# A hybrid transformer block on one core: four pieces of work set at other places

## The chip, the cores and the metric

The kernel runs as one program on one core of a Trainium2 chip. The metric is the device time of one execution in microseconds (us); less is better. The engines named below are PE (TensorE, matrix products and transposes), DVE (VectorE), ACT (ScalarE), POOL (GpSimd) and SP (SyncE, which issues nearly all transfers).

## The reference

One block of depth 1 on 512 tokens of 1024 features, in float32. What matters of it:

```python
h = layer_norm(x, emb_ln_g, emb_ln_b)
proj = h @ w_in + b_in
o_dn = gated_delta_rule(q_dn, k_dn, v_dn, beta, g)
y_dn = (rms_norm(o_dn, dn_norm_w) * silu(z)) @ w_dn_o
y_da = (rms_norm(diff_attention_alibi(q, k, v, lam), da_subln_w) * (1 - lam_init)) @ w_da_o
h = layer_norm(alpha * h + (gate_dn * y_dn + gate_da * y_da) @ w_out, ln1_g, ln1_b)
ffn = hierarchical_moe(h, ...)
ple = sigmoid(h @ w_ple_gate + b_ple_gate) * (p @ w_ple_proj)
out = layer_norm(alpha * h + ffn + ple, ln2_g, ln2_b)
```

The mixture has 16 experts, each `silu(h @ gate) * (h @ up)` with 256 inner features and then `@ down`; two experts of one group are taken per token. `p` has 256 features.

## The kernel before, in words

**Products.** A float32 product is written as three float32r products (`mm3`, L287 to L292): high part by high part, low by high, high by low. Each weight is loaded in float32 by SP and split in halves: ACT copies a half into its rounded high part (L265), DVE subtracts that to get the low part (L266). A half is 128x1024 values; one such pair of instructions is called a split here. The list `stream` (L216 to L231) gives the order of all weights from w_in on. `weights(kind, idx, loads, splits)` (L272) asks, when the program uses a weight, that the loads of the next `loads` weights and the splits of the next `splits` halves be issued.

**Order.** The program is written as Python generators whose instructions a scheduler then sets in each engine's queue; an engine works its queue in that order. A few places are pinned: under `strict` the written order holds, `behind(engine)` sets instructions behind all that went before on that engine, `issue_after` behind one instruction.

**The head.** The string `HEAD` (L487) lists tokens in a strict order on PE, DVE, ACT and POOL. Of its tokens, `l1` is one step of the p projection `ple_proj` (L329 to L357): a step makes the products of `p` with `w_ple_proj`, and ACT evicts finished banks as `PPo` (L349 for the first 128 tokens, L356 for the others), from which the three banks of the pool `pg` come free. `a0` and `q1` are the layer norm of the first 128 tokens: ACT's sum (L414) and square (L419). After them come the transposes `psh` of the normed x (L388), whose input DVE finishes at L379.

**The delta rule.** The generator `delta` (inverse, scan, then `dn_out`, L832) is woven step by step with the projections of q and k of the attention (`zqk`). For each of four groups of heads and tokens `dn_out` transposes the scan's output `OR` on PE into a bank `po` (L840), after which `split_o` makes its high and low part. `OR` of the last turn (c = 3) is scaled by `norm_o` (L751): four squares on ACT, then DVE, POOL's power `r` (L209) and DVE's product at L761. Ahead of the last turn `dn_out` waits three steps of the weave.

**The last gate.** `gate_p(c, t)` (L1062) makes the products for the gate of the p projection, four weights PG of 8x262 by four groups of tokens, with `gate_p_use` (L1074) behind them on DVE and ACT. It asks for two splits ahead.

**The experts.** For e = 0 to 15 (loop at L1399) the kernel gathers the rows of x on POOL (L1223), transposes them on PE (`psx`, L1232; ACT and DVE evict them as `xT`, L1234 and L1236), makes the 24 products `pup` of 512 columns with the two weights E(e,0) and E(e,1), gates on ACT and DVE (`eth`, L1261 to L1263), transposes the gated values (`psf`, L1268; evicted as `hT`, L1271 and L1273), and makes 12 products `pdn` with the down weight D(e). ACT evicts these as `y` (L1288) and POOL scatters `y` to `planes` in memory (L1291). There are two buffers of `y`. In `stream` D(e-1) comes behind E(e,0) and E(e,1). An expert has 4 + 2 halves to split; `up` asks for four splits ahead. The last two experts, 14 and 15 (`LAST`), scatter nothing: their results stay on the core (`ykeep`), and `load_planes` reads the planes back behind the last scatter.

Of the kernel before, what the change touches and what calls it, by code (L numbers as in the profile page):

```python
# [20 lines left out]
D = 1024  # L21
NT = 4
NE = 16
# [28 lines left out]
LOADS, SPLITS, PGL, AHEAD = 9, 4, 8, 3  # L52
# [20 lines left out]
def block_kernel(ctx, tc, x, pT, wA, wB, wO, wM, wPG, wPP, wE, wD, cols, rows, consts, out):  # L73
    nc = tc.nc
    PE, DVE, ACT, POOL = nc.tensor, nc.vector, nc.scalar, nc.gpsimd
# [17 lines left out]
    def big(shape, dt=F32, name="big"):  # L93
        return bp.tile([128] + list(shape), dt, name=nm(name), tag="B")
# [10 lines left out]
    def bank(name="ps"):  # L105
        return pt.tile([128, 512], F32, name=nm(name), tag="T")
# [13 lines left out]
    @contextmanager  # L120
    def strict(*engines):

        traced = nc.cur_bb.bb.instructions
        n0 = len(traced)
        yield
        for eng in engines:
            mine = [i for i in traced[n0:] if i.engine == eng.engine]
            for a_, b_ in zip(mine, mine[1:]):
                tc.add_manual_dep(b_, a_.name, mybir.DependencyInfo(mybir.DependencyClass.NoSync, mybir.DependencyReason.DATA),
                                  reason="program order")  # L130
# [14 lines left out]
    def behind(eng):  # L145

        return tc.issue_after(next(i for i in reversed(nc.cur_bb.bb.instructions) if i.engine == eng.engine))
# [45 lines left out]
    ident = cst[:, K_ID:K_ID + 128]  # L193
# [18 lines left out]
    stream = [("PP", 0, wPP, [2, 1024])]  # L212
# [11 lines left out]
    for c in range(4):  # L224
        stream.append(("PG", c, wPG[c], [8, 262]))
    for e in range(NE):
        stream.append(("E", (e, 0), wE[e, 0], [4, 512]))
        stream.append(("E", (e, 1), wE[e, 1], [4, 512]))
        if 0 < e:
            stream.append(("D", e - 1, wD[e - 1], [2, 1024]))  # L230
    stream.append(("D", NE - 1, wD[NE - 1], [2, 1024]))  # L231
    where = {(k, i): n for n, (k, i, _, _) in enumerate(stream)}
    raw, parts, split_at = {}, {}, {}
# [1 line left out]
    loads = []  # L235
# [4 lines left out]
    def load_to(n):  # L240
        while nload[0] < min(n, len(stream)):
            i = nload[0]
            k, _, src, shp = stream[i]
            raw[i] = big(shp, name="w" + k)
            if i:
                nc.sync.dma_start(flat(raw[i], 3), flat(src, 3))
            else:
                for j in range(2):
                    nc.sync.dma_start(raw[i][:, j], src[:, j])
            loads.append(nc.cur_bb.bb.instructions[-1])  # L250
            if i >= where["E", (FIRST, 0)]:
                tc.add_manual_dep(loads[i], loads[i - DEEP].name,
                                  mybir.DependencyInfo(mybir.DependencyClass.Sync, mybir.DependencyReason.DATA), reason="few loads in flight")
            nload[0] += 1

    def split_to(n, lo_eng=DVE):

        while nsplit[0] < min(n, 2 * len(stream)):
            i, j = divmod(nsplit[0], 2)
            k, _, _, shp = stream[i]  # L260
            load_to(i + 1)
            n2, w = shp[0] // 2, shp[1]
            r = raw[i][:, j * n2:(j + 1) * n2, :]
            hl = big([2, n2, w], F32R, name="s" + k)
            ACT.activation(hl[:, 0], r, AF.Copy)  # L265
            lo_eng.tensor_tensor(hl[:, 1], r, hl[:, 0].bitcast(F32), op=OP.subtract)  # L266
            parts[i, j] = hl
            split_at[i, j] = nc.cur_bb.bb.instructions[-2:]
            if j:
                raw.pop(i)  # L270
            nsplit[0] += 1

    def weights(kind, idx, loads=3, splits=2):

        n = where[kind, idx]
        n2 = stream[n][3][0] // 2
        load_to(n + 1 + loads)

        def get(k, sl=slice(None)):
            j, kk = divmod(k, n2)  # L280
            split_to(2 * n + j + 1 + splits)
            hl = parts[n, j]
            return hl[:, 0, kk, sl], hl[:, 1, kk, sl]
        return get
# [168 lines left out]
    def token(k):  # L453
        eng = POOL if k[-1] == "P" else DVE
        c, n = k[0], int(k.rstrip("P")[1:] or 0)
        if c == "E":
            split_emb()
        elif c == "e":
            spread_emb(n)
        elif c == "m":  # L460
            mus[n] = stats0(n)
        elif c == "p":
            split_p(eng)
        elif c == "s":
            split_to(n, eng)
        elif c == "a":
            affine(x_rows(n), mus[n], rstd0[:, n:n + 1], emb)
        elif c == "l":
            ple_steps(n)
        elif c == "u":  # L470
            sums0(n)
        elif c == "q":
            squares0(n)
        elif c == "n":
            shift0(n)
        elif c == "W":
            warm_up(n)
        elif c == "w":
            white0(n)
        elif c in "gb":  # L480
            eng.tensor_tensor(x_rows(n), x_rows(n), emb[:, c == "b", :], op=OP.mult if c == "g" else OP.add)
        elif c == "t":
            turn0(n)
        elif c == "v":
            vda(n // 10, n % 10)

    HEAD = ("E0 pP s2 e1 m0 e3 e2 e0 W3 u1 a0 q1 l1 l1 l1 l1 l1 m3 n1 t0 s3 l1 l1 l1 s4 w1 l1 l1 a3 v00 l1 l1 "  # L487
            "g1 b1 t3 l99 t1 s5 s6 v03 m2 v01 a2 v10 s7 s8 v13 t2 v11 v02 v12")
    with strict(PE, DVE, ACT, POOL):
        for k in HEAD.split():  # L490
            token(k)
# [169 lines left out]
    OR = big([4, 4, 128], name="OR")  # L661
# [162 lines left out]
    def split_o(c, po):  # L824
        tk = slice(c * 128, (c + 1) * 128)
        oh, ol = OHL[0]
        f = mid([4, 128], name="of")
        DVE.scalar_tensor_tensor(f, h4(po), dnw[:, 0:1], ZG[:, :, tk], op0=OP.mult, op1=OP.mult)
        ACT.activation(oh[:, :, tk], f, AF.Copy)
        DVE.tensor_tensor(ol[:, :, tk], f, oh[:, :, tk].bitcast(F32), op=OP.subtract)  # L830

    def dn_out():  # L832
        OHL[0] = (big([4, 512], F32R, name="OH"), big([4, 512], F32R, name="OL"))
        for c in range(4):
            if c == 3:
                for _ in range(3):
                    yield 1
            po = bank("po")
            for h in range(4):
                PE.transpose(po[:, h * 128:(h + 1) * 128], OR[:, c, h, :], ident)  # L840
            with tc.issue_after(last_square[0]):
                split_o(c, po)
            yield 1
# [216 lines left out]
    def gate_p(c, t):  # L1060
        n = PGW[c]
        c0 = sum(PGW[:c])  # L1062
        w = weights("PG", c, loads=PGL)
        tq = slice(t * 128, (t + 1) * 128)
        ps = gbank()
        steps(mm3(ps[:, :n], 8, lambda k: (cut(two(H1H, H1L, k), tq), w(k, slice(0, n)))))
        o = 20 if c == 0 else 0
        if c == 0:
            DVE.tensor_tensor(LG[:, t, :], ps[:, :20], bpg[:, 0:20], op=OP.add)
        return ps, n, o, c0  # L1070
# [575 lines left out]
```

## Time and profile before

| what | value |
| --- | --- |
| median of 3 runs | 671.49 us (670.57 to 672.28) |
| the profiled execution | 671.27 us, of it 669.5 us span |
| PE busy | 650.7 us (97%) |
| DVE busy | 496.0 us (74%) |
| ACT busy | 371.8 us (56%) |
| POOL busy | 93.8 us (14%) |
| granted clock of PE, mean | 0.995 |

The span is the time from the first to the last instruction that the profile shows. Times in the trace count from its start. PE's busy time is a modelled one, since matrix products are pipelined: a product of 512 columns is shown with 0.39 or 0.40 us, while the next one starts 0.23 us later. A row of a timeline may hold several instructions of one kind in a row (x6); its second number is then the time from the first's start to the last's end.

### The profile page before, as it was taken

How to read it: one execution, taken by the hardware profiler on the slowest of the kernel's cores; microseconds unless marked ns; L12 is line 12 of the kernel's file. 1: busy time of each engine (PE TensorE's matmuls, PEld its weight loads, DVE VectorE, ACT ScalarE, POOL GpSimd, SP SyncE). 2: the span in 40 equal slices, each digit the busy share in tenths (PEclk: the TensorE clock that was granted, in tenths of full speed). 3: DMA queues.
4: the chain of work that ended last, by engine and by line, in shares of the span. 5: the costliest groups of instructions: out<-in, count | busy, mean ns of one | idle time of the engine just before them, and what ended most of it. 6: DMA issues, size and time to landing. Idle time of an engine off the chain costs nothing.

```text
span 669.5 us, 9576 instructions
## 1 busy us (share of the span) xinstructions
PE 650.7 (97%) x3515; PEld 544.3 (81%) x3516; DVE 496.0 (74%) x922; ACT 371.8 (56%) x694; POOL 93.8 (14%) x108
## 2 busy tenths in 40 slices
PE   8999999999998999999999999999999999999993
PEld 4998888888887888888888888899978888888762
DVE  4956678995367684864726284879789999999984
ACT  6707544562466564564523232123379888989734
POOL 2000030100001212200000010200213122221310
PEclk9999999999999999999999999999999999999997
DMA  8994015113103410231611464195489999999553
GB/s 314 404 411 176 1 21 199 63 64 95 64 1 134 141 64 1 69 120 64 251 64 64 137 269 165 64 367 198 162 317 397 378 368 357 359 373 341 187 242 130
DMA packets 31764, 127.17 MB, mean 190 GB/s; under 512 B 9585, under 2 KB 11249, under 8 KB 20576
## 3 DMA queue, kind: packets, MB, share of 16 engines
q1 hardware_dynamic: 27392, 118.73, 47.2%
q0 software_dynamic: 4320, 7.77, 3.2%
q8 instruction: 29, 0.48, 0.3%
q14 instruction: 23, 0.19, 0.1%
HBM read 111.91 MB, written 22.54 MB: 201 GB/s over the span
## 4 chain that ended last, share of the span: by engine, by line
PE 58%; DVE 5%; ACT 3%; issue 1%; POOL 0%; POOLq 0%; ACTq 0%
PE pg L291 12%; PE pg L290 12%; PE pg L289 12%; PE pup L291 3%; PE pup L289 3%; PE pup L290 3%; PE pdn L291 2%; PE pdn L290 2%; PE pdn L289 2%; PE psx L1232 2%; ACT sE L265 1%; PE pov L931 1%; DVE sE L266 1%; DVE sD L266 1%; PE psc L902 1%; ACT xT L1234 1%
## 5 line engine op out<-in xcount | busy, mean ns | idle before, releaser
L289 PE MATMUL pg<-hTh,sA 128*128 128x512 f32 x320 | 129.6, 405 | 0.0
L291 PE MATMUL pg<-hTh,sA 128*128 128x512 f32 x320 | 126.8, 396 | 0.0
L290 PE MATMUL pg<-hTl,sA 128*128 128x512 f32 x320 | 126.5, 395 | 0.0
L266 DVE TENSOR_TENSOR sE<-wE,sE 128x1024 fp32r<-128x1024 f32 x64 | 75.4, 1219 | 0.3 <-ACT sE L265 0.3
L291 PEld LDWEIGHTS pg<-hTh,sA 128*128 128x128 f32 x320 | 60.2, 188 | 13.2
L289 PEld LDWEIGHTS pg<-hTh,sA 128*128 128x128 f32 x320 | 60.3, 188 | 11.5
L290 PEld LDWEIGHTS pg<-hTl,sA 128*128 128x128 f32 x320 | 60.3, 189 | 11.2
L265 ACT ACTIVATE sE<-wE 128x1024 fp32r<-128x1024 f32 x64 | 64.5, 1070 | 0.5 <-PE pg L291 0.4
L265 ACT ACTIVATE sA<-wA 128x1024 fp32r<-128x1024 f32 x40 | 41.4, 1055 | 34.7 <-PE pg L291 31.9
L266 DVE TENSOR_TENSOR sA<-wA,sA 128x1024 fp32r<-128x1024 f32 x40 | 48.7, 1225 | 6.8 <-ACT sA L265 6.6
L289 PE MATMUL pup<-sE,xT 128*128 128x512 f32 x128 | 51.6, 403 | 0.0
L290 PE MATMUL pup<-sE,xT 128*128 128x512 f32 x128 | 50.4, 394 | 0.7 <-DVE sE L266 0.7
L291 PE MATMUL pup<-sE,xT 128*128 128x512 f32 x128 | 50.4, 394 | 0.0
L266 DVE TENSOR_TENSOR sD<-wD,sD 128x1024 fp32r<-128x1024 f32 x32 | 37.8, 1220 | 3.5 <-ACT sD L265 3.3
L290 PE MATMUL pg<-sPG,H1H 128*128 128x262 f32 (+1 forms) x128 | 36.6, 286 | 0.0
L289 PE MATMUL pg<-sPG,H1H 128*128 128x262 f32 (+1 forms) x128 | 36.5, 286 | 0.0
L291 PE MATMUL pg<-sPG,H1L 128*128 128x262 f32 (+1 forms) x128 | 36.5, 285 | 0.0
L265 ACT ACTIVATE sD<-wD 128x1024 fp32r<-128x1024 f32 x32 | 32.5, 1081 | 0.0
L906 ACT ACTIVATE tt<-tt,mn 128x128 f32<-128x128 f32 (+3 forms) x32 | 17.8, 556 | 24.1 <-DVE mn L904 24.0
L1223 POOL DMA_INDIRECT xr<-h1d,ts x16 | 19.1, 1194 | 85.0 <-PE psx L1232 39.9
L530 DVE SCALAR_TENSOR_TENSOR acc<-pad,col,acc 128x512 f32<-128x512 f32 x36 | 26.7, 742 | 3.8 <-ACT acc L528 3.5
L290 PEld LDWEIGHTS pup<-sE,xT 128*128 128x128 f32 x128 | 24.1, 188 | 6.1 <-DVE sE L266 1.2
(369 smaller groups left out, 1528.2 us busy)
## 6 DMA issues: line engine op xcount, KB each, us to landing
wE<-wE SPq DMA_DIRECT2D x32, 1024.0 KB, 9.8
wA<-wA SPq DMA_DIRECT2D x20, 1024.0 KB, 5.0
wD<-wD SPq DMA_DIRECT2D x16, 1024.0 KB, 10.0
wPG<-wPG SPq DMA_DIRECT2D x4, 1048.0 KB, 7.0
planes<-nil SPq DMA_DIRECT2D x4, 1024.0 KB, 11.2
wO<-wO SPq DMA_DIRECT2D x4, 1024.0 KB, 4.8
wM<-wM SPq DMA_DIRECT2D x4, 1024.0 KB, 4.8
pl<-planes SPq DMA_DIRECT2D x4, 1024.0 KB, 10.9
```

The source lines that it names most:

```text
L265: ACT.activation(hl[:, 0], r, AF.Copy)
L266: lo_eng.tensor_tensor(hl[:, 1], r, hl[:, 0].bitcast(F32), op=OP.subtract)
L289: PE.matmul(ps, lh, rh, start=i == 0, stop=False)
L290: PE.matmul(ps, lh, rl, start=False, stop=False)
L291: PE.matmul(ps, ll, rh, start=False, stop=i == n - 1)
L530: DVE.scalar_tensor_tensor(acc, pad[:, j:j + 512], w[j], acc, op0=OP.mult, op1=OP.add)
L902: PE.matmul(ps[:, :n], qs[:, tq], kl[:, :n], start=False, stop=True)
L906: ACT.activation(tt[:, :n], tt[:, :n], AF.Exp, bias=mn[:, m:m + 1], scale=-1.0, accum_out=(s0[:, qt:qt + 1] if m == 0 else s1))
L931: PE.matmul(po[:, qt * 128:(qt + 1) * 128], aT[:, k * 128:(k + 1) * 128], VB[:, k, vo:vo + 128], start=k == 0, stop=k == qt)
L1223: POOL.indirect_dma_start(out=xr, out_offset=None, in_=h1d, in_offset=bass.IndirectOffsetOnAxis(ap=idx, axis=0), bounds_check=S - 1, oob_i ...
L1232: PE.transpose(ps[:, k * 128:(k + 1) * 128], xr[:, (kk * 4 + k) * 128:(kk * 4 + k + 1) * 128], ident)
L1234: ACT.activation(xT[:, 0, ks, :], h4(ps), AF.Copy)
```

## The change

The token string has `a0 q1` three steps `l1` later: on ACT the two evictions L349 come ahead of the square. `dn_out` waits twelve steps in place of three ahead of its last turn, and the four transposes of that turn go behind what PE then has in its queue. `gate_p` asks for four splits in place of two in its last column group (c = 3). In `stream` D(13) comes ahead of E(14,0) and E(14,1). The stream is built in one line less, so lines of the new kernel below L227 bear numbers lower by one, down to `dn_out`, where a line more evens this out.

```diff
--- before.py
+++ after.py
@@ -224,10 +224,9 @@
     for c in range(4):
         stream.append(("PG", c, wPG[c], [8, 262]))
     for e in range(NE):
-        stream.append(("E", (e, 0), wE[e, 0], [4, 512]))
-        stream.append(("E", (e, 1), wE[e, 1], [4, 512]))
-        if 0 < e:
-            stream.append(("D", e - 1, wD[e - 1], [2, 1024]))
+        ups = [("E", (e, i), wE[e, i], [4, 512]) for i in range(2)]
+        downs = [("D", e - 1, wD[e - 1], [2, 1024])] if e else []
+        stream.extend(downs + ups if e == NE - 2 else ups + downs)
     stream.append(("D", NE - 1, wD[NE - 1], [2, 1024]))
     where = {(k, i): n for n, (k, i, _, _) in enumerate(stream)}
     raw, parts, split_at = {}, {}, {}
@@ -484,7 +483,7 @@
         elif c == "v":
             vda(n // 10, n % 10)
 
-    HEAD = ("E0 pP s2 e1 m0 e3 e2 e0 W3 u1 a0 q1 l1 l1 l1 l1 l1 m3 n1 t0 s3 l1 l1 l1 s4 w1 l1 l1 a3 v00 l1 l1 "
+    HEAD = ("E0 pP s2 e1 m0 e3 e2 e0 W3 u1 l1 l1 l1 a0 q1 l1 l1 m3 n1 t0 s3 l1 l1 l1 s4 w1 l1 l1 a3 v00 l1 l1 "
             "g1 b1 t3 l99 t1 s5 s6 v03 m2 v01 a2 v10 s7 s8 v13 t2 v11 v02 v12")
     with strict(PE, DVE, ACT, POOL):
         for k in HEAD.split():
@@ -833,11 +832,12 @@
         OHL[0] = (big([4, 512], F32R, name="OH"), big([4, 512], F32R, name="OL"))
         for c in range(4):
             if c == 3:
-                for _ in range(3):
+                for _ in range(12):
                     yield 1
             po = bank("po")
-            for h in range(4):
-                PE.transpose(po[:, h * 128:(h + 1) * 128], OR[:, c, h, :], ident)
+            with behind(PE) if c == 3 else nullcontext():
+                for h in range(4):
+                    PE.transpose(po[:, h * 128:(h + 1) * 128], OR[:, c, h, :], ident)
             with tc.issue_after(last_square[0]):
                 split_o(c, po)
             yield 1
@@ -1060,7 +1060,7 @@
     def gate_p(c, t):
         n = PGW[c]
         c0 = sum(PGW[:c])
-        w = weights("PG", c, loads=PGL)
+        w = weights("PG", c, loads=PGL, splits=4 if c == 3 else 2)
         tq = slice(t * 128, (t + 1) * 128)
         ps = gbank()
         steps(mm3(ps[:, :n], 8, lambda k: (cut(two(H1H, H1L, k), tq), w(k, slice(0, n)))))
```

In the orders below each row is one instruction (or xN of them): line, operation, output<-inputs, size.

PE, at the last turn of `dn_out` (`po`, transposes of `OR`; `pg` are the products of the woven projection). Before:

```order
L291 MATMUL pg_2036<-hTh_134,sA_1825 128x512
L289 MATMUL pg_2036<-hTh_134,sA_1825 128x512
L290 MATMUL pg_2036<-hTl_136,sA_1825 128x512
L291 MATMUL pg_2036<-hTh_134,sA_1825 128x512
L289 MATMUL pg_2036<-hTh_134,sA_1825 128x512
L840 MATMUL po_2018<-cst,OR_1339 128x128 x4
L290 MATMUL pg_2036<-hTl_136,sA_1825 128x512
L291 MATMUL pg_2036<-hTh_134,sA_1825 128x512
L289 MATMUL pg_2036<-hTh_135,sA_1902 128x512
L290 MATMUL pg_2036<-hTl_137,sA_1902 128x512
L291 MATMUL pg_2036<-hTh_135,sA_1902 128x512
```

With the change:

```order
L288 MATMUL pg_2027<-hTh_135,sA_1902 128x512
L289 MATMUL pg_2027<-hTl_137,sA_1902 128x512
L290 MATMUL pg_2027<-hTh_135,sA_1902 128x512
L288 MATMUL pg_2027<-hTh_135,sA_1902 128x512
L289 MATMUL pg_2027<-hTl_137,sA_1902 128x512
L290 MATMUL pg_2027<-hTh_135,sA_1902 128x512
L840 MATMUL po_2055<-cst,OR_1339 128x128 x4
L288 MATMUL pg_2027<-hTh_135,sA_1902 128x512
L289 MATMUL pg_2027<-hTl_137,sA_1902 128x512
L290 MATMUL pg_2027<-hTh_135,sA_1902 128x512
L288 MATMUL pg_2068<-hTh_134,sA_1825 128x512
```

The last `po` stood behind the first ten of the 24 products of a tile `pg`; now it stands 11 products further on, three ahead of that tile's end.

DVE, from the last transposed rows of the experts' start to the second expert's splits (`sE` splits of E, `sD` of D, `eth` the gate of expert 0, `hT` its transposed values). Before:

```order
L1236 TENSOR_TENSOR xT_4600<-psx_4601,xT_4600 128x512
L1236 TENSOR_TENSOR xT_4600<-psx_4608,xT_4600 128x512
L266 TENSOR_TENSOR sE_4622<-wE_3905,sE_4622 128x1024
L266 TENSOR_TENSOR sE_4625<-wE_3905,sE_4625 128x1024
L266 TENSOR_TENSOR sE_4628<-wE_3907,sE_4628 128x1024
L266 TENSOR_TENSOR sE_4637<-wE_3907,sE_4637 128x1024
L266 TENSOR_TENSOR sE_4646<-wE_3909,sE_4646 128x1024
L266 TENSOR_TENSOR sE_4655<-wE_3909,sE_4655 128x1024
L1262 SCALAR_TENSOR_TENSOR eth_4664<-eth_4664,pup_4621 128x256
L1263 TENSOR_TENSOR eth_4664<-eth_4664,pup_4621 128x256
L266 TENSOR_TENSOR sD_4676<-wD_3911,sD_4676 128x1024
L266 TENSOR_TENSOR sD_4685<-wD_3911,sD_4685 128x1024
```

With the change:

```order
L1236 TENSOR_TENSOR xT_4606<-psx_4607,xT_4606 128x512
L1236 TENSOR_TENSOR xT_4606<-psx_4614,xT_4606 128x512
L1262 SCALAR_TENSOR_TENSOR eth_4664<-eth_4664,pup_4627 128x256
L1263 TENSOR_TENSOR eth_4664<-eth_4664,pup_4627 128x256
L265 TENSOR_TENSOR sE_4628<-wE_3907,sE_4628 128x1024
L265 TENSOR_TENSOR sE_4637<-wE_3907,sE_4637 128x1024
L265 TENSOR_TENSOR sE_4646<-wE_3909,sE_4646 128x1024
L265 TENSOR_TENSOR sE_4655<-wE_3909,sE_4655 128x1024
L1273 TENSOR_TENSOR hT_4703<-psf_4700,hT_4703 128x256
L265 TENSOR_TENSOR sD_4676<-wD_3911,sD_4676 128x1024
L265 TENSOR_TENSOR sD_4685<-wD_3911,sD_4685 128x1024
L265 TENSOR_TENSOR sE_4694<-wE_4023,sE_4694 128x1024
```

Two splits of expert 0 (from `wE_3905`) have gone from here to the last gate's rows, and the gate `eth` stands ahead of expert 1's four splits, no longer behind them.

DVE, from expert 13's gate to expert 15's splits (before, `wE_5649` is E(14,1) and `wD_5707` D(13); with the change `wE_5649` is E(14,0), `wE_5707` E(14,1) and D(13), `wD_5647`, stands ahead of these rows; `wE_5744` and `wE_5746` are expert 15's in both). Before:

```order
L1263 TENSOR_TENSOR eth_5877<-eth_5877,pup_5840 128x256
L266 TENSOR_TENSOR sE_5889<-wE_5649,sE_5889 128x1024
L1273 TENSOR_TENSOR hT_5910<-psf_5907,hT_5910 128x256
L1236 TENSOR_TENSOR xT_5913<-psx_5914,xT_5913 128x512
L1236 TENSOR_TENSOR xT_5913<-psx_5921,xT_5913 128x512
L266 TENSOR_TENSOR sD_5930<-wD_5707,sD_5930 128x1024
L266 TENSOR_TENSOR sD_5933<-wD_5707,sD_5933 128x1024
L266 TENSOR_TENSOR sE_5936<-wE_5744,sE_5936 128x1024
L266 TENSOR_TENSOR sE_5939<-wE_5744,sE_5939 128x1024
L266 TENSOR_TENSOR sE_5942<-wE_5746,sE_5942 128x1024
L266 TENSOR_TENSOR sE_5948<-wE_5746,sE_5948 128x1024
L1236 TENSOR_TENSOR xT_5976<-psx_5977,xT_5976 128x512
```

With the change:

```order
L1263 TENSOR_TENSOR eth_5877<-eth_5877,pup_5840 128x256
L265 TENSOR_TENSOR sE_5889<-wE_5649,sE_5889 128x1024
L1273 TENSOR_TENSOR hT_5910<-psf_5907,hT_5910 128x256
L1236 TENSOR_TENSOR xT_5913<-psx_5914,xT_5913 128x512
L1236 TENSOR_TENSOR xT_5913<-psx_5921,xT_5913 128x512
L265 TENSOR_TENSOR sE_5930<-wE_5707,sE_5930 128x1024
L265 TENSOR_TENSOR sE_5936<-wE_5707,sE_5936 128x1024
L1236 TENSOR_TENSOR xT_5964<-psx_5965,xT_5964 128x512
L1236 TENSOR_TENSOR xT_5964<-psx_5972,xT_5964 128x512
L265 TENSOR_TENSOR sE_5990<-wE_5744,sE_5990 128x1024
L265 TENSOR_TENSOR sE_5999<-wE_5744,sE_5999 128x1024
L265 TENSOR_TENSOR sE_6008<-wE_5746,sE_6008 128x1024
```

The two `sD` behind `xT` are gone (D(13) is now split ahead of this place), E(14,1)'s two `sE` stand there, and the second pair of `xT` comes ahead of expert 15's splits. On ACT, in the same place, expert 13's two evictions `y` and the `xT` of expert 15 come ahead of those splits as well:

```order
L1234 ACTIVATE xT_5913<-psx_5914 128x512
L1234 ACTIVATE xT_5913<-psx_5921 128x512
L264 ACTIVATE sE_5930<-wE_5707 128x1024
L264 ACTIVATE sE_5936<-wE_5707 128x1024
L1288 ACTIVATE y_5928<-pdn_5929,tw_4335 128x512
L1288 ACTIVATE y_5928<-pdn_5943,tw_4335 128x512
L1234 ACTIVATE xT_5964<-psx_5965 128x512
L1234 ACTIVATE xT_5964<-psx_5972 128x512
L264 ACTIVATE sE_5990<-wE_5744 128x1024
L264 ACTIVATE sE_5999<-wE_5744 128x1024
L264 ACTIVATE sE_6008<-wE_5746 128x1024
```

Before, the four splits of expert 15 stood ahead of these evictions.

## Rows read from the trace of the kernel before

**Rows 1.** Waits of PE, longest first: line waited for: us in total, times, longest.

```profile
PE po L840 <- DVE OR L761: 1.7, 1, 1.7
PE pg L289 <- ACT PPo L349: 1.4, 1, 1.4
PE pdn L289 <- ACT sD L265: 0.8, 1, 0.8
PE pup L290 <- DVE sE L266: 0.7, 1, 0.7
```

**Rows 2.** Stretches: length, busy PE, PEld, DVE, ACT, POOL (instructions), clock, DMA share, GB/s.

```profile
212.00:489.00 277.00, 277.00 (x1514) 237.99 (x1512) 182.74 (x400) 115.84 (x233) 33.80 (x31) 1.00 0.37 135
500.00:618.00 118.00, 118.00 (x573) 96.49 (x571) 114.67 (x140) 107.06 (x150) 28.82 (x23) 1.00 0.97 369
611.82:633.50 21.68, 20.63 (x97) 16.26 (x95) 21.41 (x25) 19.67 (x26) 5.03 (x5) 1.00 0.67 250
```

**Rows 3.** Timeline 11.5 to 17.5: start, us, engine, line, operation, count, idle before.

```profile
13.92 1.15 ACT L419 ACTIVATE z<-x,nmu 128x1024 f32<-128x1024 f32 x1 [0.22 <-DVE nmu L415]
15.07 1.06 ACT L349 ACTIVATE PPo<-pg 128x512 f32<-128x512 f32 x2
15.18 1.28 DVE L379 SCALAR_TENSOR_TENSOR x<-x,rstd,emb 128x1024 f32<-128x1024 f32 x1
16.52 1.09 PE L388 MATMUL psh<-cst,x 128*128 128x128 f32 x8
```

**Rows 4.** Timeline 209 to 213, PE and the DVE line it waits for.

```profile
209.32 0.39 PE L291 MATMUL pg<-hTh,sA 128*128 128x512 f32 x1
209.55 0.40 PE L289 MATMUL pg<-hTh,sA 128*128 128x512 f32 x1
210.77 0.69 DVE L761 TENSOR_TENSOR OR<-OR,r 128x512 f32<-128x512 f32 x1 [1.19 <-POOL r L209]
211.61 0.63 PE L840 MATMUL po<-cst,OR 128*128 128x128 f32 x4 [1.67 <-DVE OR L761]
```

**Rows 5.** Timeline 490 to 506, experts 0 and 1 on DVE, PE and ACT.

```profile
491.60 6.89 DVE L266 TENSOR_TENSOR sE<-wE,sE 128x1024 fp32r<-128x1024 f32 x6
491.74 0.40 PE L289 MATMUL pup<-sE,xT 128*128 128x512 f32 x1
495.82 0.40 ACT L1261 ACTIVATE eth<-pup 128x256 f32<-128x256 f32 x1
498.41 0.42 DVE L1262 SCALAR_TENSOR_TENSOR eth<-eth,pup 128x256 f32<-128x256 f32 x1
498.86 0.42 DVE L1263 TENSOR_TENSOR eth<-eth,pup 128x256 f32<-128x256 f32 x1
499.43 0.41 PE L1268 MATMUL psf<-cst,eth 128*128 128x128 f32 x2 [0.28 <-DVE eth L1263]
505.00 0.41 DVE L1263 TENSOR_TENSOR eth<-eth,pup 128x256 f32<-128x256 f32 x1
505.51 0.39 PE L1268 MATMUL psf<-cst,eth 128*128 128x128 f32 x2
```

**Rows 6.** Timeline 635 to 638: expert 15's gate, with nothing ahead of it.

```profile
635.76 0.40 PE L291 MATMUL pup<-sE,xT 128*128 128x512 f32 x1
636.19 0.39 ACT L1261 ACTIVATE eth<-pup 128x256 f32<-128x256 f32 x1 [1.71 <-PE pup L291]
637.07 0.42 DVE L1263 TENSOR_TENSOR eth<-eth,pup 128x256 f32<-128x256 f32 x1
```

**Rows 7.** Timeline 618 to 634, the last experts on PE and DVE.

```profile
633.10 0.41 DVE L1263 TENSOR_TENSOR eth<-eth,pup 128x256 f32<-128x256 f32 x1
633.65 0.41 PE L1268 MATMUL psf<-cst,eth 128*128 128x128 f32 x2 [0.22 <-DVE eth L1263]
```

**Rows 8.** Expert 11's scatter on POOL, and its time from issue to landing.

```profile
614.12 0.99 POOL L1291 DMA_INDIRECT planes<-y,tdi  x1 [8.48 <-ACT sE L265]
planes<-y,tdi POOLq DMA_INDIRECT x1, 8.7
```

## The prediction

> **What bounds the kernel now.** I read the list of waits first, then stretches, then the timeline at each place that the change touches. PE is busy 97% of the span, so only its waits can be won. The list names the four that the change aims at [rows 1]: the transposes `po` 1.7 us, the p projection 1.4, the down product of expert 13 0.8, the up product of expert 0 0.7. The stretches show what lies between: from 212 to 489 and from 500 to 618 PE is busy for the whole length [rows 2]. So what PE gains before such a stretch is carried through it, if nothing else is as tight. In the expert loop something is: DVE works 114.67 of 118 us there, and 21.41 of the 21.68 us from 611.82 to 633.50, where PE works only 20.63 [rows 2]. There the reader is to see two engines level, with DVE the tighter at the end.
>
> The sum below is made against the profiled execution (671.27 us, span 669.5); the median of the runs, 671.49, is 0.22 above it.
>
> **1. The evictions `PPo` ahead of the square: 0.** ACT begins the square at 13.92 and the two evictions at 15.07, which take 1.06 [rows 3]. With the evictions first they start no later than 13.92 and end by 14.98, so the three products that waited 1.4 us run over 1 us sooner. But the transposes `psh` that follow on PE need x, which DVE finishes at 15.18 + 1.28 = 16.46, and they start at 16.52 [rows 3]. DVE's order there is the same, so they still do. The wait moves from ahead of the products to behind them. Bounds: 0, and -1.4 if the transposes could start earlier; I take 0, since the row of x excludes the other. The square ends some 1.1 later, about 16.2, which still lies in front of the 16.46 at which DVE is free.
>
> **2. The last `po` 11 products later: -1.83.** Products of 512 columns start 0.23 us apart (209.32, 209.55); the last before the wait starts at 209.55, `po` at 211.61, 2.06 later [rows 4]. A turn without a wait would have come 0.23 later, so 1.83 is lost. Now 11 more products, 2.53 us, lie in between: PE comes to `po` at 209.55 + 0.23 + 2.53 = 212.31, and `OR` is ready at 210.77 + 0.69 = 211.46 [rows 4]. It has 0.8 us to spare. On ACT, DVE and POOL nothing is ahead of `OR` that was not before. Behind it, the scaling and splitting of `po` come later; their users are PE products several us on. PE is full from 212 to 489 [rows 2], so the 1.83 arrive at the experts. Bounds: -1.83, and 0 if DVE's later `of` held the next projection tile up; I take -1.83, since 0.8 us are spare.
>
> **3. Four splits ahead in the last gate: +1.4.** Before, DVE makes six splits in a row, 6.81 us from 491.60 to 498.41, that is 1.135 each, and then expert 0's gate; PE loses 0.9 at its 14th product of expert 0 (0.7 idle and a slow restart) and 0.45 at `psf` (499.43) [rows 1, 5]. The two splits of E(0,1) now lie in the last gate, where DVE is idle a third of the time (182.74 of 277 us busy from 212 to 489 [rows 2]), at no cost. But on ACT and DVE expert 0's gate now stands ahead of the four splits of expert 1. The gate can't start before PE's last product: the 13th of 24 starts at 491.74 [rows 5], so the 24th, without a stall, 11 times 0.23 later, at 494.27. Expert 15's gate has nothing ahead of it and shows the chain: ACT starts 0.43 after the last product, DVE's second operation 0.88 later and takes 0.42 [rows 6]. So `eth` is ready at about 496.0, and `psf` starts at 496.1, 1.6 after its slot, rather than 499.43. DVE has had nothing to do for 3.4 us from 491.6 to 495.1, and only then makes the four splits, 4.54 us. From one gate's second operation to the next were 505.00 - 498.86 = 6.14 us of full work [rows 5], which now has the four splits in it too: expert 1's gate comes at 495.6 + 4.54 + 6.14 = 506.3, with 0.1 for ACT's first copy 506.4, against 505.00. `psf` of expert 1 follows at 506.9 instead of 505.51 [rows 5]: 1.4 later. From there PE is the bound again as before. Bounds: -1.35 (both losses gone, if the gate's place cost nothing) and +1.4; I take +1.4, since both engines work in order: `eth` was copied by ACT at 495.82 and DVE came to it only at 498.41, behind its splits [rows 5].
> The Trainium skill, "PSUM — Partial Sum Buffer", section "Engine vs sequencer instructions", says that ScalarE's and VectorE's queues are strictly first in, first out; the trace agrees with the 498.41 just named. By that rule the term is +1.4; could an engine pass over the waiting gate, it would be -1.35.
>
> **4. D(13) ahead of E(14): +1.2.** PE's wait of 0.8 for `sD` [rows 1] goes, since D(13) is split before PE comes to it. But `psf` of expert 14 at 633.65 waits for DVE's `eth` at 633.10 [rows 7], and DVE makes as many splits ahead of it as before, in another order. From 611.82 it has only 0.27 us idle to lose [rows 2]; so at best -0.3. At worst: expert 13's evictions and the `xT` of expert 15 now stand on ACT ahead of expert 15's splits. The evictions need one of the two buffers of `y`, that of expert 11, whose scatter is issued at 614.12 and lands 8.7 us later, at 622.8 [rows 8]. PE finishes the first half of the products by then. Two evictions of the size of those at 15.07 (1.06 [rows 3]) and one `xT` of about 0.6, being of the same size as one eviction, put DVE's `xT` at about 624.6. DVE is free for it at 623.6: 633.10 less seven splits (7.95), two `xT` and one step of the gate (1.5 together, as I estimate them from their widths beside a split's). With one more gap of 0.25 before those splits, which wait for ACT in turn, that is 1.25; without the scatter's part 0.55. I take 1.2, because the scatter's row gives the later end. What follows `psf` is a chain of DVE and PE to the end, so it moves with it.
>
> **Sum:** 0 - 1.83 + 1.4 + 1.2 = +0.8: 671.27 to 672.1 for the profiled execution, 672.3 for the median. No measurement of this kernel can tell less than about 0.3%, 2.0 us, from no change: I forecast no change.
>
> **The rivals.**
> A. As above, +0.2 (the scatter costs nothing) to +1.5: 671.5 to 673.2, **0.50**.
> B. All as meant: places 2, 3 and 4 gain and no order costs anything, -1.83 - 1.35 - 0.3 = -3.5, 668.0. For it: each wait aimed at is real [rows 1]. Against it: the in-order queues of place 3, and a DVE without idle time at the end. **0.12**, faster.
> C. Only one of places 3 and 4 costs: -1.83 + 1.4 - 0.3 = -0.7 or -1.83 - 1.35 + 1.2 = -2.0, 669.5 to 670.8. **0.18**, nearly all of it no change.
> D. The scatter of expert 11 lands later. Each us more holds up expert 13's evictions, with them all later copies on ACT, and so `psf` of expert 14 by a us. By the order on SP the loads of `at`, four of 512 KB, now wait for E(13,1)'s products in place of D(12)'s, 12 products or 2.8 us sooner, and so share the DMA engines (0.97 busy in the loop [rows 2]) with that scatter. From a landing 1.2 us later than 622.8 on, 9.9 us after its issue, the sum passes +2.0; twice that gives +3.2, 674.7. For it: the queues are full; against it: behind the last weight loads the engines have less to do, 0.67 from 611.82 on [rows 2]. **0.20**, most of it slower.
> That place 2 does not do what it says (the later `po` meets a late `OR`) would need `OR` 0.8 us later than now, with nothing new ahead of it; it is left inside D's share, at +1.8.
>
> **The numbers.** The likeliest is A, 672.3. The range leaves out B and the far part of D, 0.19 together: 669.5 to 674.2. Faster by over 0.3% is B and the edge of C, 0.15; slower is most of D, 0.19; between them 0.66.
>
> **What would show it.** Right: `psh` still at 16.5, now with about 1 us idle ahead of it and no wait for `PPo`; no wait for `OR`; no wait of `pup` for a split in expert 0, but waits of 1.6 and about 1.3 us at the first two `psf`, with DVE idle some 3.4 us ahead of the first gate; no wait of `pdn` for `sD`; a wait of 1.5 to 2.6 us at `psf` of expert 14, with ACT's `y` of expert 13 released by POOL's scatter. Wrong: DVE busy through 491 to 495; `psf` of expert 14 earlier, by the trace, than 1.8 us before 633.65; a `psh` earlier than 16.4; or time lost between 212 and 489.

## The result and the profile after

The change is slower: 675.24 us (median of 4 runs, 673.50 to 676.44) against 671.38 (4 runs of the kernel before beside them, 670.57 to 672.28), a ratio of 1.0055 with a 95% interval of 1.0029 to 1.0081 (the numbers in brackets behind later ratios are such intervals). The forecast, 672.3 in a range of 669.5 to 674.2, lies below it. The profiled execution alone, at 673.50, would have lain inside. That execution (span 671.7) is the fastest of the four; against the 671.27 of before it is 2.23 later. So the trace below shows less than the median lost, and a second trace of the same kernel, further down, shows the rest.

The waits of PE in the changed kernel, in the form of [rows 1] (line waited for: us in total, times, longest); the last row is the wait for the gates in the kernel before:

```profile
PE psf L1268 <- DVE eth L1263: 4.7, 3, 2.1
PE pzt L1505 <- DVE st L1492: 2.0, 3, 1.2
PE psh L387 <- DVE ss L419: 0.3, 1, 0.3
PE psf L1268 <- DVE eth L1263: 0.7, 3, 0.3
```

All four waits of [rows 1] are gone, as they were meant to be. In their place the wait for the gates at `psf` has grown from 0.7 to 4.7 us, in three pieces. The wait at `pzt` is the same before. Down to `dn_out`, line numbers are one less than before.

**Place 1.** Timeline of the head (start, us, engine, line, operation, count, idle before), beside [rows 3]:

```profile
14.35 1.09 ACT L348 ACTIVATE PPo<-pg 128x512 f32<-128x512 f32 x2 [0.21 <-PE pg L345]
15.62 1.28 DVE L378 SCALAR_TENSOR_TENSOR x<-x,rstd,emb 128x1024 f32<-128x1024 f32 x1
16.24 0.40 PE L290 MATMUL pg<-sPP,ptl 128*128 128x512 f32 x1
16.96 0.77 PE L387 MATMUL psh<-cst,x 128*128 128x128 f32 x5 [0.32 <-DVE ss L419]
```

The products run on without a stop to 16.24, and `psh` still stands behind x: 15.62 + 1.28 = 16.90. This execution's x came 0.44 later than in [rows 3], and so did `psh`; the idle time ahead of `psh` is 0.32, where about 1 us was named.

**Place 2.** PE at the last `po`, and DVE's `OR`, beside [rows 4]:

```profile
211.16 0.69 DVE L760 TENSOR_TENSOR OR<-OR,r 128x512 f32<-128x512 f32 x1 [1.19 <-POOL r L209]
212.49 0.39 PE L290 MATMUL pg<-hTh,sA 128*128 128x512 f32 x1
212.72 0.60 PE L840 MATMUL po<-cst,OR 128*128 128x128 f32 x4
```

`OR` is ready at 211.85 and `po` follows its product by 0.23 at 212.72: no wait.

**Place 3.** The first two experts, beside [rows 5]:

```profile
492.77 0.40 PE L290 MATMUL pup<-sE,xT 128*128 128x512 f32 x1
493.61 0.42 DVE L1262 SCALAR_TENSOR_TENSOR eth<-eth,pup 128x256 f32<-128x256 f32 x1 [3.44 <-ACT eth L1261]
494.56 4.63 DVE L265 TENSOR_TENSOR sE<-wE,sE 128x1024 fp32r<-128x1024 f32 x4
494.64 0.41 PE L1268 MATMUL psf<-cst,eth 128*128 128x128 f32 x2 [1.47 <-DVE eth L1263]
504.92 0.41 DVE L1263 TENSOR_TENSOR eth<-eth,pup 128x256 f32<-128x256 f32 x1
505.38 0.44 PE L1268 MATMUL psf<-cst,eth 128*128 128x128 f32 x2 [1.09 <-DVE eth L1263]
```

PE's 24th product of expert 0 is at 492.77, where [rows 5] with their stall taken out gave 494.27: 1.50 us sooner, about the 1.83 of place 2 less the 0.44 by which the head was late. Then DVE stands idle for 3.44 us, does the gate, and only now the four splits. At the second `psf` 505.38 is left against 505.51: the 1.5 us won are spent.

**Place 4.** The last gates on ACT, DVE and PE, beside [rows 6, 7]:

```profile
622.18 1.27 ACT L1288 ACTIVATE y<-pdn,tw 128x512 f32<-128x512 f32 x2
623.97 1.29 DVE L1236 TENSOR_TENSOR xT<-psx,xT 128x512 fp32r<-128x512 f32 x2 [0.40 <-ACT xT L1234]
634.35 0.41 PE L1268 MATMUL psf<-cst,eth 128*128 128x128 f32 x2 [2.10 <-DVE eth L1263]
637.20 0.63 PE L289 MATMUL pup<-sE,xT 128*128 128x512 f32 x1
637.62 0.63 PE L290 MATMUL pup<-sE,xT 128*128 128x512 f32 x1
639.16 0.42 DVE L1263 TENSOR_TENSOR eth<-eth,pup 128x256 f32<-128x256 f32 x1
```

`psf` of expert 14 is 0.70 later than in [rows 7], inside what was forecast. But the last `eth` is 2.09 later than in [rows 6] (637.07). Between the two stand products that start 0.42 us apart (637.20, 637.62) where they are 0.23 apart elsewhere. The stretches say why (length, busy PE, PEld, DVE, ACT, POOL, clock, DMA share, GB/s); the last row is the kernel before:

```profile
634.50:636.00 1.50, 1.50 (x7) 1.21 (x7) 1.17 (x2) 0.39 (x1) 1.50 (x2) 0.68 1.03 421
636.00:638.50 2.50, 2.50 (x8) 1.93 (x7) 0.00 (x0) 0.21 (x1) 2.50 (x4) 0.51 1.03 426
636.00:638.50 2.50, 2.50 (x13) 2.00 (x12) 1.02 (x3) 1.29 (x3) 2.50 (x4) 1.00 0.98 406
```

PE's granted clock is 0.51 there, the lower of its two levels (1.2 of 2.4 GHz), behind a wait of 2.10 us. In the kernel before the same stretch has 1.00. The last gate is 1.4 us later by it (2.09 less 0.70), and no term of the sum held that.

### The profile page after: what moved, and what is told of

It reads as the page before. It is cut to its first block, busy times and chain, and to the rows that moved or that the text cites. A ratio compares the mean times of both kernels' runs of the same rounds, so it can differ in the third digit from the quotient of the medians.

```text
span 671.7 us, 9575 instructions
## 1 busy us (share of the span) xinstructions
PE 652.8 (97%) x3515; PEld 547.4 (81%) x3516; DVE 496.3 (74%) x922; ACT 371.5 (55%) x694; POOL 96.3 (14%) x108
## 4 chain that ended last, share of the span: by engine, by line
PE 86%; DVE 7%; ACT 3%; DMA 1%; issue 1%; POOL 0%; SPq 0%; POOLq 0%; DVEq 0%; ACTq 0%
PE pg L290 19%; PE pg L288 19%; PE pg L289 19%; PE pup L290 4%; PE pup L288 3%; PE pup L289 3%; DVE sE L265 2%; PE psx L1232 2%; PE pdn L288 2%; PE pdn L290 2%; PE pdn L289 2%; PE pov L931 1%; DVE sD L265 1%; DMA wPP<-wPP 1%; PE psh L387 1%
## 5 line engine op out<-in xcount | busy, mean ns | idle before, releaser
L288 PE MATMUL pup<-sE,xT 128*128 128x512 f32 x128 | 52.3, 408 | 0.0
L290 PE MATMUL pup<-sE,xT 128*128 128x512 f32 x128 | 51.2, 400 | 0.0
L289 PE MATMUL pup<-sE,xT 128*128 128x512 f32 x128 | 50.9, 397 | 0.0
L1291 POOL DMA_INDIRECT planes<-y,tdi x14 | 20.3, 1447 | 74.8 <-ACT sD L264 31.6
## 6 DMA issues: line engine op xcount, KB each, us to landing
planes<-nil SPq DMA_DIRECT2D x4, 1024.0 KB, 12.1
```

The costliest lines, as they stand in the source:

```text
L288: PE.matmul(ps, lh, rh, start=i == 0, stop=False)
L289: PE.matmul(ps, lh, rl, start=False, stop=False)
L290: PE.matmul(ps, ll, rh, start=False, stop=i == n - 1)
L1291: POOL.indirect_dma_start(out=planes, out_offset=bass.IndirectOffsetOnAxis(ap=idxs, axis=0), in_=y, in_offset=None, bounds_check=2 * S - 1 ...
```

## The experiments

Each ratio is to runs of the kernel before on the same chip: 670.81 us (24 runs) for places 2, 3 and 4 alone and the change again, 670.82 (27) for the other buffer, the filled wait and the first two mended versions, 671.06 (23) for place 1 alone and the third mended version, 670.67 (23) for the pairs of places and the change with a later gate.

### Each place alone

Each kernel is the one before with one hunk of the diff. Place 2:

```diff
-                for _ in range(3):
+                for _ in range(12):
...
+            with behind(PE) if c == 3 else nullcontext():
```

> Only the last turn of dn_out twelve steps on. Theory (the parts add up as the trace of the change shows them): the wait for OR (1.7 idle) is gone, the 1.8 us arrive at the experts, 669.5 to 669.8 where before is 671.4. Rival (the tail cannot use it, since the planes are read back behind a chain of scatters that transfers pace): the experts begin 1.8 us sooner and the end moves by less than 0.6.

Measured: 668.96 (8 runs), ratio 0.9971 (0.9961 to 0.9982), -1.85 us. The term was -1.83.

Place 3:

```diff
-        w = weights("PG", c, loads=PGL)
+        w = weights("PG", c, loads=PGL, splits=4 if c == 3 else 2)
```

> Only four splits ahead in the last gate. Theory: no wait of pup for a split, psf of expert 0 waits 1.5 idle, expert 1's gate 1.4 us later than before, so +1.4, about 672.8, clock 1.00 behind that wait. Rival (the clock falls to half behind this wait in some executions, which would be the 1.8 us that the other runs of the change had more than the profiled one): +2.5 to +3.5, 674 to 675, in part of the runs.

Measured: 672.23 (9 runs), 1.0027 (1.0016 to 1.0039), +1.4 us. The clock stayed at 1.00 behind the wait of 1.5 us. The term was +1.4.

Place 4:

```diff
+        ups = [("E", (e, i), wE[e, i], [4, 512]) for i in range(2)]
+        downs = [("D", e - 1, wD[e - 1], [2, 1024])] if e else []
+        stream.extend(downs + ups if e == NE - 2 else ups + downs)
```

> Only D(13) ahead of E(14). Theory: psf of expert 14 about 0.8 us later than before because of DVE's new gaps, its wait about 2.1 us idle in place of 0.2, and behind it some eight products at half clock, 1.4 us: +2.2, about 673.6. Rival (the clock fell only because three places together left PE idle): psf 0.8 later, clock 1.00 behind it, +0.8, 672.2.

Measured: 672.99 (12 runs, 671.34 to 677.62), 1.0039 (1.0018 to 1.0060), +2.2 us as expected, though not in the parts expected: the profile, of an execution of 672.96 near the middle of this spread, shows `psf` at 633.79 with 1.87 idle ahead of it, only 0.14 later than in [rows 7]; the clock behind it is

```profile
636.00:638.50 2.50, 2.50 (x7) 1.97 (x6) 0.84 (x2) 0.38 (x1) 2.50 (x5) 0.50 1.00 423
```

so nearly all of that execution's loss against the 671.27 of before is the half clock. What the runs of 675.8 and more lost, no profile shows.

Place 1 (the token string of the change alone; its expectation uses other words for it):

```diff
-... W3 u1 a0 q1 l1 l1 l1 l1 l1 m3 ...
+... W3 u1 l1 l1 l1 a0 q1 l1 l1 m3 ...
```

> Only the evictions of the expansion, the p projection and the gate set sooner, on the stream of before. Theory (the prediction's place 1: the first hidden products wait for the x transposes' last copy, whatever the evictions do): no difference, 670.5 to 671.2. Rival: an eviction that ends sooner lets the hidden products begin sooner, 0.3 to 1 us faster.

Measured: 670.74 (11 runs) against 671.06, ratio 1.0000 (0.9991 to 1.0009): nothing, as the term said.

The four together are 0 - 1.85 + 1.4 + 2.2 = +1.75. The change, unaltered, was measured again beside the parts:

> The change itself once more, to see a second profile of it. Theory (the first trace is typical, +2.2): 673.5 to 674, losses at expert 0's psf and behind expert 14's psf alone. Rival (a further loss of some 1.8 us that the first trace did not hold): 675 to 676, with a place of low clock or a wait that the first trace does not show; the stretches of the new trace against the first will name it.

Measured: 676.00 (6 runs), 1.0067 (1.0053 to 1.0080), +5.2 us. Its trace, of an execution of 677.17, shows what the first one, of 673.50, could not (timeline of ACT, DVE and PE):

```profile
625.12 1.27 ACT L1288 ACTIVATE y<-pdn,tw 128x512 f32<-128x512 f32 x2 [3.49 <-DMA planes<-y,tdi]
626.91 1.29 DVE L1236 TENSOR_TENSOR xT<-psx,xT 128x512 fp32r<-128x512 f32 x2 [3.83 <-ACT xT L1234]
637.28 0.66 PE L1268 MATMUL psf<-cst,eth 128*128 128x128 f32 x2 [4.15 <-DVE eth L1263]
```

ACT's eviction of expert 13 waits 3.49 us for the scatter of expert 11, and PE 4.15 us at `psf`. This is the wait of rival D. The clock is 0.62 in the six us from 634, and 0.50 from 640 to 642.

### Taking away the wait for the scatter, and filling PE's wait

The first is the change with another buffer for expert 13's output rows, so that no scatter holds it up; the second is the change with ten products ahead of `psf`, in the same bank, where the transposes overwrite them.

```diff
+             y=XR[e % NX] if e == NE - 3 else None)
```

```diff
+            for _ in range(fill):
+                PE.matmul(ps, hl[:, 0, 0, :128], hl[:, 0, 0, :], start=True, stop=True)
```

> The change, but expert 13's result goes to the gather buffer of its own rows, long read by then, and so waits for no scatter. Theory (the scatter of expert 11 holds ACT up, by 0.1 us in the change's first trace and 3.5 in its second): ACT's y of expert 13 follows its products, psf of expert 14 waits about 1.5 us idle in every run, 672.5 to 673.5 where the change has 675 to 676, and a narrower spread. Rival (the order of DVE's splits alone sets that psf): within 0.5 of the change.

Measured: 671.22 (11 runs), 1.0008 (0.9999 to 1.0016). Some 4 us of the change's loss (3.9 and 5.2 us in its two measurements, 0.4 here) go with that buffer, more than expected. In this profile they are the wait for the scatter and the half clock together. The wait that is left, and the clock behind it:

```profile
633.78 0.41 PE L1268 MATMUL psf<-cst,eth 128*128 128x128 f32 x2 [1.86 <-DVE eth L1263]
636.00:638.50 2.50, 2.50 (x14) 1.94 (x13) 0.89 (x3) 1.15 (x3) 2.50 (x5) 1.00 1.02 429
```

(a row of the timeline, and one of the stretches). After 1.86 us idle the clock is full here, after 1.87 it was half with place 4 alone: these rows do not say what decides near that length.

> The change, with ten products of 512 columns (2.3 us) put on PE ahead of the psf of expert 14, into its bank, where PE otherwise waits; their result is overwritten. Theory (the wait itself makes the clock fall): the products behind psf are 0.23 us apart instead of 0.43, clock 1.00 from 634 to 640, 1.4 to 1.9 us less than the change, 674 to 674.5. Rival (the clock falls there for another reason, of the DMA load or of the place in the program): still 0.43 apart, and up to 0.3 us slower than the change.

Measured: 673.06 (12 runs), 1.0037 (1.0021 to 1.0052), +2.2 us where the change has +3.9 and +5.2, so 1.6 to 3 us less, and below the theory's 674. The fill, the wait left behind it, and the clock:

```profile
623.24 1.27 ACT L1292 ACTIVATE y<-pdn,tw 128x512 f32<-128x512 f32 x2 [1.65 <-DMA planes<-y,tdi]
631.56 2.44 PE L1270 MATMUL psf<-sE 128*128 128x512 f32 x10
635.31 0.44 PE L1272 MATMUL psf<-cst,eth 128*128 128x128 f32 x2 [1.31 <-DVE eth L1263]
...
636.00:638.50 2.50, 2.50 (x12) 2.04 (x12) 0.94 (x3) 0.56 (x2) 2.50 (x4) 1.00 1.03 433
```

The scatter was waited for as before; with PE kept busy the clock stayed at 1.00, though `psf` comes later than with place 4 alone. So here PE's idle time, not the late gate, decides the clock. This rests on one profile with the fill, and the 1.86 us above show that not every such wait has the half clock behind it.

### One account of all these traces

The rest of the time is the time of the execution less the start of `psf`.

| profiled execution | `y` of expert 13 starts (ACT) | `psf` of expert 14 starts (PE) | rest of the time | clock, 634 to 640 |
|---|---|---|---|---|
| before, 671.27 | 625.93 | 633.65 | 37.62 | 1.00 |
| change, 673.50 | 622.18 | 634.35 | 39.15 | 0.72 |
| change again, 677.17 | 625.12 | 637.28 | 39.89 | 0.62 |
| place 4 alone, 672.96 | 621.72 | 633.79 | 39.17 | 0.72 |
| other buffer, 671.41 | 621.71 | 633.78 | 37.63 | 1.00 |
| filled wait, 672.88 | 623.24 | 635.31 | 37.57 | 1.00 |

With place 4 `psf` comes 12.1 us (12.07 to 12.17) behind the eviction each time, so each us that the eviction is late is one of PE. The rest of the time is 37.6 us with the full clock and 39.1 to 39.9 with the half. In the kernel before the eviction stood behind four splits, so that a scatter that landed before 625.93 was waited for by nobody (landed 622.83, by [rows 8]):

```profile
625.93 1.26 ACT L1288 ACTIVATE y<-pdn,tw 128x512 f32<-128x512 f32 x2
```

Place 4 took that cover of 3.8 us away.

### Which place makes the scatter late

The parts do not add up to the whole. Rows of POOL, which issues the scatters, show a candidate: in five of the six profiles that have place 3 with expert 0's gate ahead of expert 1's splits, the issue of expert 1's scatter takes 4.8 to 5.5 us. The sixth is the first trace of the change, with 1.0. The timeline's rows of it and of DVE beside it, in the change again and then in the first trace:

```profile
516.93 2.35 DVE L265 TENSOR_TENSOR sD<-wD,sD 128x1024 fp32r<-128x1024 f32 x2
517.35 5.10 POOL L1291 DMA_INDIRECT planes<-y,tdi  x1 [3.88 <-ACT sD L264]
519.20 2.35 DVE L265 TENSOR_TENSOR sE<-wE,sE 128x1024 fp32r<-128x1024 f32 x2
```

```profile
517.29 1.01 POOL L1291 DMA_INDIRECT planes<-y,tdi  x1 [3.31 <-ACT sD L264]
517.45 2.35 DVE L265 TENSOR_TENSOR sD<-wD,sD 128x1024 fp32r<-128x1024 f32 x2
```

These rows also show what goes with the length. The long issue begins 0.42 us into a split on DVE and ends 0.90 behind the fourth of the splits in a row (519.20 + 2.35 = 521.55, against 522.45); the short one begins 0.16 ahead of the first of them. All fifteen profiles agree: each of the 115 scatter issues of more than 1.1 us begins inside a split and ends 0.84 to 0.90 us behind the end of one, and none of the other 95 begins inside a split, save in its first 0.02 or last 0.23 us. So the same order of instructions gives either length, by a few tenths of a us. No run varied this alone, and why five issues wait for four splits where most wait for one stays open.

Expert 2's scatter follows at 530.81 there and at 526.19 here, and each scatter is issued only when the one before has landed (0.7 to 0.8 us behind it wherever the landing can be read). At the end of the chain the lag has become smaller: expert 11's scatter is issued at 615.36 to 616.75 in the five profiles with the long issue, at 610.55 to 614.12 in nine of the ten others, and at 617.38 in the tenth, place 2 alone.

> Places 2 and 4 without place 3. In four of the five profiles that have place 3 with expert 0's gate ahead of expert 1's splits, the issue of the second scatter takes POOL 4.8 to 5.5 us (1.0 in those without it) and it lands some 13 us after its start, so that all later scatters come some 4 us later. Theory (what the parts don't add up to comes of this stall, so of place 3 beside place 4): no stall, ACT's eviction of expert 13 waits little or not, 670.0 to 671.5. Rival (it comes of place 2, which brings TensorE earlier against scatters that keep their pace): 672.5 or more, with that eviction waiting 2 us or more for a scatter.

> Places 3 and 4 without place 2. Theory (place 3's stall beside place 4): as much above the sum of the two parts alone (674.4) as the whole change is, 676.5 to 678, with the second scatter's issue at 5 us on POOL. Rival (place 2 beside place 4): 674 to 675, no more than the two parts.

Measured: places 2 and 4, 671.29 (12 runs), 1.0007 (0.9991 to 1.0022), +0.6 where the parts give +0.35. Places 3 and 4, 676.39 (6 runs), 1.0083 (1.0069 to 1.0096), just under the theory's range, +5.7 where the parts give +3.6. So the excess, 2 us here, is of place 3 beside place 4, not of place 2: taking place 2's 1.85 off the 5.7 gives +3.9, which is what the change had at first (3.86; its second measurement, +5.2, has 3.4 us above the parts). Without place 3 (first fence) and without place 2 (second):

```profile
514.98 1.02 POOL L1291 DMA_INDIRECT planes<-y,tdi  x1 [3.30 <-ACT sD L264]
620.93 1.27 ACT L1288 ACTIVATE y<-pdn,tw 128x512 f32<-128x512 f32 x2 [1.08 <-PE psx L1232]
633.09 0.41 PE L1268 MATMUL psf<-cst,eth 128*128 128x128 f32 x2 [3.15 <-DVE eth L1263]
```

```profile
518.25 5.36 POOL L1290 DMA_INDIRECT planes<-y,tdi  x1 [3.63 <-ACT sD L264]
624.92 1.27 ACT L1287 ACTIVATE y<-pdn,tw 128x512 f32<-128x512 f32 x2 [2.16 <-DMA planes<-y,tdi]
637.08 0.41 PE L1267 MATMUL psf<-cst,eth 128*128 128x128 f32 x2 [4.18 <-DVE eth L1262]
```

Again 12.16 us from eviction to `psf` in both. The third run sets expert 0's gate behind expert 1's splits in the whole change:

```diff
+            with tc.issue_after(split_at[n, 1][0]), tc.issue_after(split_at[n, 1][1]):
+                gate(th, ps)
```

> The whole change with expert 0's gate set behind expert 1's splits, nothing else mended. Theory (the gate ahead of the splits brings both the 1.4 us and the stall of the second scatter, and the stall the long wait at the last gate): the stall is gone, 669.5 to 671.0. Rival (the wait at the last gate is place 4's own): 672 or more, the 1.4 us and the 1.3 us of a missing first wait won and the long wait kept.

Measured: 671.13 (12 runs, 667.97 to 673.74), 0.9998 (0.9980 to 1.0017), a little above the theory's range. The stall is gone (issue 1.0 us, at 512.75), and still its profile, of 673.74, has the long wait:

```profile
622.55 1.26 ACT L1295 ACTIVATE y<-pdn,tw 128x512 f32<-128x512 f32 x2 [4.41 <-DMA planes<-y,tdi]
634.61 0.41 PE L1275 MATMUL psf<-cst,eth 128*128 128x128 f32 x2 [2.49 <-DVE eth L1270]
636.00:638.50 2.50, 2.50 (x7) 1.93 (x6) 0.00 (x0) 0.00 (x0) 2.50 (x5) 0.50 1.01 423
```

(the last is of the stretches). PE comes earlier here (its second `psf` is at 501.40, in [rows 5] at 505.51), the scatters at the end do not, so the eviction waits 4.41 us though the landing is no later than before. Both views hold in part: the stall makes the landing late, and work that is won ahead of the scatters is waited away at them. How much of the change's spread (673.5 to 677.2) is the stall was not measured alone: expert 11's scatter landed at 620.8 and at 625.0 in profiles without it as well.

### Versions with the places mended

Places 2 and 3 with expert 0's gate set later; then the whole change with that, the other buffer, and expert 14's gate set behind expert 15's splits; then the first with expert 14's gate set so, without place 4.

```diff
-            with behind_split(LAST[1]):
+            with behind_split(LAST[0], j=0):
```

> Places 2 and 3 alone, with the gate of expert 0 set behind expert 1's four splits on ACT and DVE. Theory (the gate's place in those queues was the loss of place 3): no wait of PE in expert 0, none at its psf, which now comes 20 products later, nor at expert 1's; 1.8 + 1.35 = 3.1 us won by then, 667.7 to 668.7 in all, if the end lets some of it through. Rival (place 3 wins nothing because DVE is the bound from there on): as place 2 alone, 669.0.

> The change with three things mended: the gate of expert 0 behind expert 1's splits, expert 13's result in the gather buffer, and the gate of expert 14 behind expert 15's splits but ahead of D(14)'s (hT of expert 14 behind D(14)'s first). Theory: psf of expert 14 waits for nothing, clock 1.00 to 655, 3.1 us won at the experts' start and about 1 at their end: 666.5 to 667.5. Rival (the chain of scatters, each issued when the one before has landed, holds the reading of the planes and with it the end): a wait of DVE for the planes, 668 to 669.

> The last po 22 products later and four splits before the last gate as in the change, the gate of expert 0 behind expert 1's splits, the gate of expert 14 behind expert 15's splits, and D(13) left behind E(14) as before (no place 4). Theory (the wait for the last scatters is only what place 4 and the 1.8 us gained ahead of it bring; with D(13) late the chain of scatters and the reading of the planes hold nothing): as places 2 and 3 with the gate set later, 668.3, or up to 0.5 us less. Rival (the reading of the planes holds the end also without place 4): 668.3 or more, with VectorE's additions of the planes waited for at the end.

Measured: 668.33 (8 runs), 0.9963 (0.9953 to 0.9973); 668.29 (6 runs), 0.9963 (0.9951 to 0.9975); 669.48 (12 runs), 0.9976 (0.9964 to 0.9988). The first two are faster than both kernels, by 2.5 us against the one before, and not told apart from each other. The first lies in its theory's range; the second was expected at 666.5 to 667.5 and came out as its rival said. The third is no better (-1.6 us against the runs beside it), so its theory missed and its rival held. In place of the waits at the gates stands one at the end, here of the second of them (waits of DVE, then of PE, then DVE's first addition of a plane):

```profile
DVE at L1357 <- DMA pl<-planes: 2.7, 1, 2.7
```

```profile
PE plast L1487 <- DVE ykeep L1291: 3.0, 2, 2.4
```

```profile
636.88 1.22 DVE L1357 TENSOR_TENSOR at<-at,pl 128x1024 f32<-128x1024 f32 x1 [2.69 <-DMA pl<-planes]
```

The planes are read back when the last scatter has landed, and DVE's additions wait for them; in the kernel before the first such addition started at 639.32 and waited for nothing. It starts 2.44 earlier, and the execution (668.61) ended 2.66 earlier. With places 2 and 3 mended and in the third kernel DVE waits 2.4 us there as well, so also without place 4: with the gates mended the reading of the planes is the next bound.

## Why the prediction was wrong

- **Place 1, 0: right.** `psh` starts 0.06 behind the end of x, as its row said; alone the place measures 0.
- **Place 2, -1.83: right.** -1.85 alone, and no wait for `OR`. Its 0.8 us to spare was 0.87 in the trace (212.72 less 211.85).
- **Place 3, +1.4: right in its size, and incomplete.** Alone +1.4; in the change's first trace DVE is idle for 3.44 us where 3.4 was forecast, with waits of 1.47 and 1.09 at the two `psf` (1.6 and about 1.3). What the step left out was POOL: the scatters. It followed ACT, DVE and PE, but not the indirect transfers that the first evictions trigger, and with place 4 behind it this is worth 2 us and more.
- **Place 4, +1.2: the step that failed.** Its chain was right: from a landing at 622.8 it gave `psf` at 634.9, 12.1 us behind it, and 12.1 is what all profiles with place 4 and the last gate in its place show. In the first trace the eviction started at 622.18 and the delay was 0.70. Two things were wrong. First, the landing was taken as fixed at the one value of [rows 8]; in the changed kernel the eviction had to wait until 625.12 in the second trace, +3.6 for `psf`. That was rival D, given 0.20, whose 674.7 stands nearest to the 675.24. The mechanism named there, loads of `at` that share the DMA engines, is not what the traces show: the loads do come sooner (615.36 and 614.85 in the change's two traces, 618.22 before), but expert 11's scatter takes 8.5 us to land in both, no more than the 8.7 before. In the second trace it is issued later instead, at 616.50 (613.56 in the first, 614.12 before), behind the second scatter's long issue and the chain of scatters. Second, "what follows `psf` is a chain of DVE and PE to the end, so it moves with it": it moved and became longer. Behind the wait PE's clock was at half, 1.5 to 2.3 us in the column of the table, and no term or rival held that. The term of +1.2 measured +2.2 alone, and 2.1 to 3.4 us more beside place 3.
- **The sum:** with 0, -1.85, +1.4 and +2.2 as measured it is +1.75, 673.2 for the median of before, inside the range. The rest, 2.1 us in the first measurement and 3.4 in the second, is places 3 and 4 together. Two smaller slips changed no step: rival A's own terms, +0.2 to +1.5, give 671.7 to 673.0 on the median and not 671.5 to 673.2; and the runs did tell less than 2.0 us from nothing, since the interval of place 3's +1.4 leaves out 1.
- **Of what would show it:** the named signs came, the wait of 1.5 to 2.6 us at `psf` of expert 14 among them (2.10), with two exceptions: `psh` had 0.32 us idle ahead of it in the first trace (1.33 in the second) where about 1 was named, and the trace names a scatter as what released the eviction only in the second. The sum was judged from signs that PE's clock does not enter.

## What to carry to other kernels

Before an eviction or a copy is moved ahead of other work, look what that work covered: here 3.8 us of splits hid a scatter's landing, and without them each us of its lateness was one of the whole. A transfer's landing in one trace is one draw (here 622.1 and 625.0 in two traces of one kernel); where the path comes to hang on it, take it from several, and take work that is won ahead of a chain of transfers as won only if that chain moves too. A wait that PE gets in exchange for others can cost twice, as it did in most profiles here, once as idle time and once in the products behind it: price those at either clock.

## What was not expected of the hardware

- Idle waits of PE of 1.87, 2.10, 2.49, 3.15, 4.15 and 4.18 us at the same place were followed by products 0.43 us apart, at a granted clock near 0.5 for 2 us and more; waits of 1.47 at the first expert and 1.86 in the same place as the 1.87 were not. The length of one wait does not decide it: in the change with a later gate, two waits of 0.99 and 0.77 us at 625.78 and 627.04 had products 0.43 us apart and a clock of 0.50 from 628.5 to 631 behind them. Ten products of no use in front of the wait, 2.44 us, had a clock of 1.00 behind them, and the kernel with them was faster than the change.
- POOL's issue of one indirect scatter took 1.0 us in some executions and 4.8 to 5.5 in others, among them two of one kernel (1.01 and 5.10), and where it was long the next scatter came some 4 to 6 us later than in the first trace. All long issues begin while DVE is at a split and end 0.84 to 0.90 us behind the end of one.
